# Input projection of a hybrid encoder layer: the last ten blocks as five pairs with seven products for eight, output gates stored to DRAM, second norms paced anew

## The chip, the cores and the metric

The kernel runs on one core of a Trainium2 chip. The metric is the time of one execution on the device in microseconds; the value compared is the median of the runs. The core's engines are TensorE (PE in the profile, its weight loads PEld), VectorE (DVE), ScalarE (ACT), GpSimd (POOL) and SyncE (SP), which issues nearly all DMAs.

## The reference

One layer of a chunk-causal encoder, on 1024 prompt tokens and 32 sample tokens (1056 columns, T) with 1024 features, in float32:

```python
h = rmsnorm(x, g_mix) * (1 + sc1) + sh1
u = h @ w_in
qa, ka, va, qm, km, vm, om, ip, fp, ga, gm = jnp.split(u, _split_points(), axis=-1)
ya = prompt_band_attention(qa, ka, va, rel_bias)       # 8 heads x 64
hm, (C1, n1, m1) = mlstm_chunkwise(q_m, k_m, v_m, log_i, log_f, C0, n0, m0, block)
ym = (head_rmsnorm(hm, mh_gain) * jax.nn.sigmoid(om)).astype(dt)   # 4 heads x 128
merged = (jax.nn.sigmoid(ga) * (ya @ w_br_att)
          + jax.nn.sigmoid(gm) * (ym @ w_br_mlstm))
x = x + gt1 * (merged @ w_out)
h2 = rmsnorm(x, g_ffn) * (1 + sc2) + sh2
g, up = jnp.split(h2 @ w_gate_up, 2, axis=-1)
x = x + gt2 * ((jax.nn.silu(g) * up) @ w_down)         # then a last rmsnorm
```

The change touches the columns `om` (512), `ga` and `gm` (1024 each) of `h @ w_in`, and the pace of `h2`'s norm.

## The kernel before, in words

Features lie on the partitions, tokens along the free axis, in three tiles of 352 (`TILES`). Every float32 operand is split into a high and a low part (`split_to`: ACT copies the high one, DVE or POOL subtracts for the low one), and a product is three passes (`PASSES`: high x high, low x high, high x low). `hs` holds the eight chunks of 128 features of `h`, split.

The input projection is cut into blocks of 128 output columns. A block calls `unit` once for each token tile: 8 chunks x 3 passes = 24 matmuls into one PSUM buffer from `mmt()` (three buffers, tag `mm`), and then ACT copies the buffer out: `om_block` into a slot (line 1324), `gate_block` into `raw` (line 747), which SP stores to `g_d` in DRAM. Other blocks serve attention, the convolution and the values of the mLSTM.

`segs` lists the blocks in seven segments. Beside the blocks of a segment runs a side job, a generator whose steps `Side.tick` calls in equal distances; `unit` ticks after every second chunk, that is every six matmuls. A side step issues its instructions at that place of the code: each engine but SP works in the order of the code. The last segment (index 6) has four `om_block`s and eight `gate_block`s; its job is the second half of the mLSTM, then `branch_operands`, with a delay of 13 ticks:

```python
ticks = sum(4 * run.w[2] for run in blocks)
delay = 13 if i >= 5 else 0
job = side.start(gen(), steps, ticks - delay - 4, delay)
```

The mLSTM goes over nine token blocks in steps: `first` (scores and transposes on PE, weights on DVE and ACT), `second` (four matmuls each with the state, the keys and the weights; ACT scales `num`, DVE adds and inverts, ACT squares) and, two iterations on, `third` (transposes into an `mm` buffer, copied out by ACT). The adaLN job (`ada_rest`, line 1298) runs beside all of it on DVE. `branch_operands` makes `ym` (sigmoid of `om` on ACT, line 1331; product with the mLSTM's output on DVE, line 1332; split) and `ya` (load of `ya_d`, line 1343; split). These go into the pool `slots`, 16 buffers of [128, 2, 1056]; `tmp` has four of [128, 1056].

`Weights` loads, splits and hands out the weights ahead of PE: `W.use` issues the splits of up to `W.ahead` blocks that fit in four split tiles (`wsp`), and loads three blocks ahead (`wraw`, three buffers).

After the projection the branches are merged with `sigmoid(ga)`, `sigmoid(gm)` from `g_d`. The output projection is partly in pairs of blocks with seven products for eight (`out_pair`, `half`, line 2011), whose results DVE adds to the residual (`take`, line 1946). `second_norm` makes `h2` beside it, for the first tile and then for the other two: `statistics` sums squares on PE (lines 1769, 1771), `spread` broadcasts the root, and then eight steps normalise one chunk each.

Of the kernel before, what the change touches and what calls it, by code (L numbers as in the profile page):

```python
# [17 lines left out]
P = 128  # L18
# [121 lines left out]
def hybrid_stream_step(  # L140
# [53 lines left out]
    def f(ap):  # L194
        return ap.bitcast(F32)
# [1114 lines left out]
    ADA_STEPS = 138  # L1310


    om = [None, None]
    ym, ya = [], []

    def om_block(b):
        w = w_cols(OM + b * P)

        def run():
            if b % 2 == 0:  # L1320
                om[b // 2] = slot([P, 2, T])
            for lo, hi in TILES:
                pt = unit(w, 0, hs, lo, hi)
                act.activation(om[b // 2][:, b % 2, lo:hi], pt, AF.Copy)
        run.w = w
        return run

    def branch_operands():
        for b in range(4):
            o = om[b // 2][:, b % 2]  # L1330
            act.activation(o, o, AF.Sigmoid)
            dve.tensor_tensor(o, o, hm_n[b // 2][:, b % 2], op=ALU.mult)
# [5 lines left out]
        if "ym" in dbg:  # L1338
            for h in range(MH):
                sp.dma_start(dbg["ym"][h], om[h // 2][:, h % 2])  # L1340
        for b in range(4):
            raw = tmpt()
            sp.dma_start(raw, ya_d[b])
            y = slot([P, 2, T], F32R)
            split_to(y, raw)
            ya.append(y)
            yield

    BR_STEPS = 12
# [22 lines left out]
    def open_mls():  # L1372
        att_cm.__exit__(None, None, None)
        mls_cm = tc.tile_pool(name="mls", bufs=2)
        mp_t.append(mls_cm.__enter__())
        mp_t.append(mls_cm)
        maskbig = mp_t[0].tile([P, P], F32, tag="maskbig", name="maskbig", bufs=1)
        pool.memset(maskbig, 0.0)
        pool.affine_select(out=maskbig, in_=maskbig, compare_op=ALU.is_ge, fill=BIG, base=0,
                           pattern=[[1, P]], channel_multiplier=-1)  # L1380
        masks.append(maskbig)

    def conv_rows():
        yield
        for out, j in ((new_conv_p, 0), (new_conv_s, 3)):
# [9 lines left out]
         lambda: attention(3), ATT_STEPS),  # L1395
        (open_mls, [vm_block(1), conv_block(2), conv_block(6), conv_block(3), conv_block(7)],
         lambda: mlstm(0), ML_STEPS),
        (nothing, [om_block(b) for b in range(4)] + b_gates(8, 16),
         lambda: chain(mlstm(1), conv_rows(), branch_operands()), ML_STEPS + BR_STEPS + 3),
    ]  # L1400

    for _, blocks, _, _ in segs:
        for run in blocks:
            W.add(run.w)


    class Seven:
# [610 lines left out]
    def out_pair(j, u):  # L2018
# [20 lines left out]
        if j == 1:  # L2039
# [592 lines left out]
```

## Time and profile before

| | |
|---|---|
| Median of 3 runs | 1580.81 us (1579.87 to 1581.0) |
| The profiled execution | 1580.16 us, of which the trace's span is 1578.4 us |
| Granted TensorE clock, mean | 0.999 |
| PE busy | 1558.0 us (99%), 10133 matmuls |
| DVE, ACT, POOL busy | 1133.5 (72%), 800.1 (51%), 422.7 (27%) us |
| First `om_block` | first evacuation at 545.9 us |
| Last `gate_block` | last evacuation at 701.8 us |
| HBM read, written | 149.06 MB, 34.17 MB |

Times in the profile are microseconds from the start of the span unless marked ns. A row names the line of the kernel, engine, operation, output <- input by the program's names, shape and count. In a list in order of time the first two columns are start and duration, and brackets give the time for which the engine was idle just before and what ended it. Matmuls are pipelined: the duration of one reaches into the next.

### The profile page before, as it was taken

Reading aid. Unit: us, or ns where it says so; the run is one execution under the profiler, and the core shown is the slowest. Engines: PE = TensorE matmul, PEld = TensorE weight load, DVE = VectorE, ACT = ScalarE, POOL = GpSimd, SP = SyncE. Lnnn points to the kernel's source line nnn. Section 1 sums busy time; section 2 is a strip of 40 time slices with the busy share of each in tenths; the row PEclk is TensorE's granted clock in tenths of the full one; section 3 lists DMA queues with packets and bytes.
Section 4 is the critical chain, followed back from the end, with each engine's and each line's share of the span. In section 5 each row is a group of like instructions: output and inputs, shape, how many; then the busy total and the mean of one; then the engine's idle time right before and its main releaser. Section 6 shows DMA issues by size and latency. Waiting matters only on the chain.

```text
span 1578.4 us, 27250 instructions
## 1 busy us (share of the span) xinstructions
PE 1558.0 (99%) x10133; PEld 1540.7 (98%) x10133; DVE 1133.5 (72%) x2346; ACT 800.1 (51%) x1756; POOL 422.7 (27%) x434
## 2 busy tenths in 40 slices
PE   8999999999999999999999999999999999999997
PEld 8999999999999999999999999999999999999997
DVE  3865565556766845546796799888888988799755
ACT  4765454544555545444454746544544445545443
POOL 0433343342223411000013100665665650000000
PEclk9999999999999999999999999999999999999999
DMA  9322233333132322573453312223222227427444
GB/s 375 128 78 83 89 97 103 97 131 108 42 91 74 85 81 86 126 233 131 128 163 123 108 55 68 82 69 103 72 82 95 68 78 256 143 81 244 139 135 159
DMA packets 173474, 184.99 MB, mean 117 GB/s; under 512 B 11830, under 2 KB 138458, under 8 KB 173214
## 3 DMA queue, kind: packets, MB, share of 16 engines
q1 hardware_dynamic: 171078, 182.13, 36.5%
q8 instruction: 80, 1.31, 0.3%
q10 hardware_dynamic: 2264, 1.13, 0.3%
q14 instruction: 52, 0.43, 0.1%
HBM read 149.06 MB, written 34.17 MB: 116 GB/s over the span
## 4 chain that ended last, share of the span: by engine, by line
PE 88%; DVE 5%; ACT 3%; DMA 2%; issue 1%; POOL 0%; DVEq 0%; SPq 0%; ACTq 0%; POOLq 0%
PE mm L418 37%; PE psb L2146 18%; PE mm L2146 11%; PE psb L2545 3%; PE mm L971 3%; PE mm L2545 2%; PE psV L876 2%; PE psb L2410 2%; PE mm L2011 2%; PE psS L817 1%; DMA s<-in_w_ada_dram 1%; PE psT L844 1%; PE mm L2410 1%; DMA s<-in_x_dram 1%; DVE st L831 1%
## 5 line engine op out<-in xcount | busy, mean ns | idle before, releaser
L418 PE MATMUL mm<-s,wsp 128*128 128x352 f32 x3720 | 625.2, 324 | 0.3 <-DVE s L688 0.3
L418 PEld LDWEIGHTS mm<-s,wsp 128*128 128x128 f32 x3720 | 595.5, 188 | 2.1 <-DVE s L688 0.5
L381 DVE TENSOR_TENSOR wsp<-wraw,wsp 128x512 fp32r<-128x512 f32 (+1 forms) x260 | 216.4, 849 | 94.5 <-ACT wsp L380 92.6
L2146 PE MATMUL psb<-s,wsp 128*128 128x352 f32 x1581 | 266.7, 322 | 0.0
L380 ACT ACTIVATE wsp<-wraw 128x512 fp32r<-128x512 f32 (+1 forms) x316 | 188.3, 617 | 136.2 <-PE psb L2146 42.0
L2146 PEld LDWEIGHTS psb<-s,wsp 128*128 128x128 f32 x1581 | 255.9, 188 | 0.0
L2146 PE MATMUL mm<-s,wsp 128*128 128x352 f32 x945 | 161.5, 322 | 0.7 <-DVE row L2184 0.7
L2146 PEld LDWEIGHTS mm<-s,wsp 128*128 128x128 f32 x945 | 153.2, 188 | 1.1 <-ACT wsp L380 1.0
L837 POOL TENSOR_SCALAR st<-st,mx 128x640 f32<-128x640 f32 (+5 forms) x72 | 53.2, 739 | 182.9 <-DVE mx L836 164.9
L1298 DVE CUSTOM_DVE_ANT_0 junk<-wa,t 128x512 bf16<-128x512 f32 x128 | 94.6, 739 | 2.5 <-DMA wa<-in_w_mod_dram 1.4
L381 POOL TENSOR_TENSOR wsp<-wraw,wsp 128x512 fp32r<-128x512 f32 x56 | 74.8, 1355 | 51.6 <-ACT wsp L380 49.3
L831 DVE CUSTOM_DVE_ANT_0 st<-psS,bias 128x640 f32<-128x640 f32 (+5 forms) x72 | 44.5, 618 | 57.9 <-PE psS L817 41.2
L832 ACT ACTIVATE st<-st,mx 128x640 f32<-128x640 f32 (+5 forms) x72 | 47.9, 666 | 63.7 <-DVE mx L831 63.5
L1961 POOL TENSOR_TENSOR t<-t,sl 128x352 f32<-128x352 f32 x19 | 22.7, 1198 | 207.2 <-ACT sl L1959 207.1
L851 ACT ACTIVATE pT<-psT 128x640 fp32r<-128x640 f32 (+3 forms) x80 | 38.6, 493 | 64.2 <-PE psT L844 49.8
L2518 POOL TENSOR_TENSOR fst<-fst,mhalf 128x6 f32<-128x6 f32 x1 | 2.2, 2247 | 235.2 <-DVE fst L2517 235.2
L856 DVE TENSOR_TENSOR pT<-psT,pT 128x640 fp32r<-128x640 f32 (+3 forms) x80 | 44.0, 558 | 21.5 <-ACT pT L851 21.5
L1511 POOL TENSOR_TENSOR wraw<-wraw,raw 128x512 f32<-128x512 f32 x33 | 55.8, 1702 | 0.9
L380 ACT ACTIVATE s<-x 128x352 fp32r<-128x352 f32 x84 | 37.5, 487 | 35.4 <-DVE x L1747 35.4
L971 PE MATMUL mm<-s,s 128*128 128x264 f32 (+3 forms) x432 | 54.5, 283 | 0.0
L2545 PE MATMUL psb<-s,wsp 128*128 128x352 f32 x330 | 54.1, 323 | 0.0
L2545 PEld LDWEIGHTS psb<-s,wsp 128*128 128x128 f32 x330 | 53.1, 188 | 0.1
(406 smaller groups left out, 2666.2 us busy)
## 6 DMA issues: line engine op xcount, KB each, us to landing
wraw<-in_w_in_dram SPq DMA_DIRECT2D x37, 512.0 KB, 3.7
wraw<-in_w_gate_up_dram SPq DMA_DIRECT2D x33, 512.0 KB, 4.1
wa<-in_w_mod_dram SPq DMA_DIRECT2D x64, 256.0 KB, 2.8
wraw<-in_w_down_dram SPq DMA_DIRECT2D x32, 512.0 KB, 4.1
a_d<-t SPq DMA_DIRECT2D x22, 528.0 KB, 2.7
g_d<-t SPq DMA_DIRECT2D x16, 528.0 KB, 3.4
t<-g_d SPq DMA_DIRECT2D x16, 528.0 KB, 4.6
s<-in_w_ada_dram SPq DMA_DIRECT2D x16, 512.0 KB, 7.9
```

The costliest lines, as they stand in the source:

```text
L380: act.activation(dst[:, 0], src, AF.Copy)
L381: eng.tensor_tensor(dst[:, 1], src, f(dst[:, 0]), op=ALU.subtract)
L418: pe.matmul(pt[:, :hi - lo], wt[(w0 + k) // 4][:, a, (w0 + k) % 4], xt[k][:, b, lo:hi], start=(k == 0 and q == 0), stop=(k == n - 1 and q ...
L831: dve.tensor_tensor_reduce(so, sv, bi, -1.0, 3.0e38, ALU.add, ALU.min, mx[:n, 1:2])
L832: act.activation(st[:n, :w], st[:n, :w], AF.Exp, bias=mx[:n, 1:2], scale=-1.0, accum_out=mx[:n, 2:3])
L837: pool.tensor_scalar(st[:n, :w], st[:n, :w], mx[:n, 3:4], 1.0, op0=ALU.mult, op1=ALU.mult)
L971: pe.matmul(pt[:n, :wd], hs[k][:, a, i * P:i * P + n], whl[b][:, k, :wd], start=(k == 0 and q == 0), stop=(k == KD - 1 and q == 2))
L1298: dve.tensor_tensor_reduce(junk, wa, crow[:, c], 1.0, 0.0, ALU.mult, ALU.add, at)
L1511: self.eng.tensor_tensor(a(dst), a(x), a(y), op=op)
L2146: pe.matmul(acc, wt[:, a, k], x[k][:, b], start=(start and not onto and k == 0 and q == 0), stop=(stop and k == 3 and q == 2), skip_group_ ...
L2410: pe.matmul(acc, wt[k // 4][:, u, k % 4], piece_of[k, i][:, v], start=(k == 0 and q == 0), stop=(k == KP - 1 and q == 2))
L2545: pe.matmul(acc, wt[(k - k0) // 4][:, u, (k - k0) % 4], piece_of[k, 2][:, v], start=(k == 0 and q == 0), stop=(k == NF - 1 and q == 2))
```

## The change

Om blocks 2 and 3, and for j = 4 to 7 the blocks j of `ga` and `gm`, become five pairs. In a pair, with its two weight blocks a and b, the feature chunks 0, 1, 4, 5 (`X`) on the token tiles 1 and 2 are a 2 x 2 by 2 x 2 product of blocks (each two chunks deep), done by seven products with sums of weights and of tokens instead of eight. Chunks 2, 3, 6, 7 (`R`), and tile 0, are multiplied as before. The token sums `T1` to `T4` are made once, beside om blocks 0 and 1 (`input_forms`: POOL joins high and low parts, DVE subtracts, ACT and DVE split), and live in a new pool `tf` of four buffers and in two slots. The weight sums are made by DVE for every pair.

A partial sum `u` stays in one PSUM buffer through the whole pair and is read after each of its products; `v` likewise for a shorter time. Om columns go to `om_d` in DRAM and are loaded again by `branch_operands`, one step ahead of their sigmoid. `W.ahead` is 4 from this segment on. The first `second_norm` waits one step less after its sums and makes 11 steps in 31 ticks with a delay of 1 (before: 12 in 28 with 2); the second starts one tick later.

```diff
     def om_block(b):
...
         def run():
-            if b % 2 == 0:
-                om[b // 2] = slot([P, 2, T])
+            raw = tmpt()
             for lo, hi in TILES:
                 pt = unit(w, 0, hs, lo, hi)
-                act.activation(om[b // 2][:, b % 2, lo:hi], pt, AF.Copy)
+                act.activation(raw[:, lo:hi], pt, AF.Copy)
+            sp.dma_start(om_d[b], raw)
...
     def branch_operands():
+        om = []
         for b in range(4):
-            o = om[b // 2][:, b % 2]
+            if b % 2 == 0:
+                om[:] = [slot([P, 2, T])]
+                sp.dma_start(om[0], om_d[b:b + 2].rearrange("n p t -> p n t"))
+                yield
+            o = om[0][:, b % 2]
             act.activation(o, o, AF.Sigmoid)
...
-    BR_STEPS = 12
+    def input_forms():
+        early, mid, late = [slice(lo, hi) for lo, hi in TILES]
+        places = [tf_pool[0].tile([P, 2, NT], F32R, tag="tf", name=nm("tf")) for _ in range(4)]
+        for n in (3, 1):
+            t = slot([P, 2, T], F32R)
+            places += [t[:, :, slice(lo, hi)] for lo, hi in TILES[:n]]
...
+        for p in range(2):
+            x = tmpt((P, 3, NT))
+            x0, x1, x2 = (x[:, i] for i in range(3))
+            whole(x0, p, mid)
+            whole(x2, p, late)
+            yield
+            whole(x1, p + 4, mid)
+            yield
+            minus(x2, x0, x2)
+            minus(x0, x1, x0)
+            yield
+            split("T1", p, x2)
+            minus(x1, x1, x2)
+            yield
+            split("T2", p, x1)
...
+    FORM_STEPS = 19
+    class InputSeven:
...
+            def sums():
+                x.append(tmpt((P, 4, 2, P)))
+                s1, s2, s3, s4 = (x[0][:, i] for i in range(4))
+                for o, u, v, op in ((s1, a(1, 0), a(1, 1), ALU.add), (s2, s1, a(0, 0), ALU.subtract),
+                                    (s3, a(0, 0), a(1, 0), ALU.subtract), (s4, a(0, 1), s2, ALU.subtract)):
+                    dve.tensor_tensor(o, u, v, op=op)
...
+    def input_pair(ca, cb, da, db):
...
+        def product(w, x, acc, i=0, start=True, stop=True, onto=False):
+            wt, = W.use(w)
+            n = len(x)
+            for k in range(n):
+                for q, (a, b) in enumerate(PASSES):
+                    pe.matmul(acc, wt[:, a, i + k], x[k][:, b], ...)
+                if k % 2 == 1:
+                    side.tick()
+            side.flush(1)
+            W.used(w)
+            return acc
...
+            u = product(aX, h((0, 1), t2), new())
+            copy(ra[:, t2], u)
+            c = product(aX, h(X, t0), new(), stop=False)
+            product(aR, h(R, t0), c, start=False)
+            copy(ra[:, t0], c)
+            c = product(aX, h((4, 5), t2), new(), 2, stop=False)
+            product(aR, h(R, t2), c, start=False)
+            add(ra[:, t2], c)
+            product(s12, F["T2"], u, 2, onto=True)
+            copy(ra[:, t1], u)
+            c = product(aR, h(R, t1), new())
+            add(ra[:, t1], c)
+            v = product(s12, F["T1"], new())
+            copy(rb[:, t1], v)
+            product(s34, F["T3"], u, onto=True)
+            add(rb[:, t1], u)
+            product(s34, h((4, 5), t1), v, 2, onto=True)
+            add(ra[:, t1], v)
+            sp.dma_start(da, ra)
+            c = product(bX, h(X, t0), new(), stop=False)
+            product(bR, h(R, t0), c, start=False)
+            copy(rb[:, t0], c)
+            product(bX, F["T4"], u, 2, stop=False, onto=True)
+            product(bR, h(R, t2), u, onto=True)
+            copy(rb[:, t2], u)
+            c = product(bR, h(R, t1), new())
+            add(rb[:, t1], c)
+            sp.dma_start(db, rb)
+        run.ticks = 23
...
+    BR_STEPS = 14
...
-        (nothing, [om_block(b) for b in range(4)] + b_gates(8, 16),
+        (nothing, [om_block(0), om_block(1), input_pair(OM + 2 * P, OM + 3 * P, om_d[2], om_d[3])]
+         + [input_pair(GA + j * P, GM + j * P, g_d[2 * j], g_d[2 * j + 1]) for j in range(4, 8)],
          lambda: chain(mlstm(1), conv_rows(), branch_operands()), ML_STEPS + BR_STEPS + 3),
...
+        if i == 6:
+            W.ahead = 4
+            side.start(input_forms(), FORM_STEPS, 21)
...
-            jobs.append(side.start(second_norm(parts[0], 2), 12, 28, 2))
+            jobs.append(side.start(second_norm(parts[0], 1), 11, 31, 1))
...
-                job = side.start(chain(second_norm(parts[1]), early_forms()), 9, 10)
+                job = side.start(chain(second_norm(parts[1]), early_forms()), 9, 10, 1)
```

More of the change, by code (lines that the diff above doesn't have):

```diff
@@ L1310, in hybrid_stream_step @@
     ADA_STEPS = 138
-    om = [None, None]
+    om_d = dr.tile([4, P, T], F32, name="om_d")
     ym, ya = [], []
@@ L1337, in branch_operands @@
             yield
-        if "ym" in dbg:
-            for h in range(MH):
-                sp.dma_start(dbg["ym"][h], om[h // 2][:, h % 2])
         for b in range(4):
@@ new lines, in hybrid_stream_step, with __init__, load, a @@
+    FORM_STEPS = 19
+    class InputSeven:
+        def __init__(self, ca, cb):
+            raw, x = [], []
+            def load(c):
+                raw.append(wraw.tile([P, KD, P], F32, tag="wraw", name=nm("wraw")))
+                sp.dma_start(raw[-1], in_block(c))
+            def a(i, h):
+                return raw[i][:, 4 * h:4 * h + 2]
+            def rows(i, g):
+                return raw[i].rearrange("p (h g k) c -> p h g k c", h=2, g=2)[:, :, g]
+            def sums():
[4 more added lines that the diff above has]
+                    dve.tensor_tensor(o, u, v, op=op)
+                return x[0][:, 0:2]
+            def block(src, uses, ld=lambda: None):
+                def split(_):
+                    t = wsplit_tile()
+                    v = src()
+                    hi, lo = (t[:, i].rearrange("p (h k) c -> p h k c", h=2) for i in range(2))
+                    act.activation(hi, v, AF.Copy)
+                    dve.tensor_tensor(lo, v, f(hi), op=ALU.subtract)
+                    return [t]
+                return [ld, split, uses, None, 1]
+            self.blocks = [
+                block(lambda: rows(0, 0), 3, lambda: load(ca)),
+                block(lambda: rows(0, 1), 3, lambda: load(cb)),
+                block(sums, 2),
+                block(lambda: x[0][:, 2:4], 2),
+                block(lambda: rows(1, 0), 2),
+                block(lambda: rows(1, 1), 3),
+            ]
@@ new lines, in input_pair, with h, new, run @@
+    def input_pair(ca, cb, da, db):
+        seven = InputSeven(ca, cb)
+        t0, t1, t2 = [slice(lo, hi) for lo, hi in TILES]
+        X, R = (0, 1, 4, 5), (2, 3, 6, 7)
+        def product(w, x, acc, i=0, start=True, stop=True, onto=False):
[3 more added lines that the diff above has]
+                for q, (a, b) in enumerate(PASSES):
+                    pe.matmul(acc, wt[:, a, i + k], x[k][:, b], start=(start and not onto and k == 0 and q == 0),
+                              stop=(stop and k == n - 1 and q == 2), skip_group_check=onto)
+                if k % 2 == 1:
[3 more added lines that the diff above has]
+            return acc
+        def h(ks, t):
+            return [hs[k][:, :, t] for k in ks]
+        def new():
+            return mmt()[:, :NT]
+        def run():
+            aX, aR, s12, s34, bX, bR = seven.blocks
+            F = forms_h
+            ra, rb = tmpt(), tmpt()
+            def add(o, y):
+                dve.tensor_tensor(o, o, y, op=ALU.add)
+            def copy(o, y):
+                act.activation(o, y, AF.Copy)
+            u = product(aX, h((0, 1), t2), new())
[26 more added lines that the diff above has]
+            sp.dma_start(db, rb)
+        run.blocks = seven.blocks
+        run.ticks = 23
+        return run
@@ L1376, in open_mls @@
         mp_t.append(mls_cm)
+        tf_cm = tc.tile_pool(name="tf", bufs=4)
+        tf_pool[:] = [tf_cm.__enter__(), tf_cm]
         maskbig = mp_t[0].tile([P, P], F32, tag="maskbig", name="maskbig", bufs=1)
@@ L1403, in hybrid_stream_step @@
         for run in blocks:
-            W.add(run.w)
+            for w in getattr(run, "blocks", None) or [run.w]:
+                W.add(w)
     class Seven:
@@ L1690, in hybrid_stream_step @@
         if gen is not None:
-            ticks = sum(4 * run.w[2] for run in blocks)
+            ticks = sum(getattr(run, "ticks", None) or 4 * run.w[2] for run in blocks)
             delay = 13 if i >= 5 else 0
@@ L1699, in hybrid_stream_step @@
     side.flush()
+    tf_pool[1].__exit__(None, None, None)
     mp_t[1].__exit__(None, None, None)
```

27 lines of the change are left out of this document (added).

## The prediction

> **What bounds the kernel now.** I read the busy shares first, then the stretches of time, then the waits of TensorE (PE) in the one stage that the change rewrites, then the engines in order of time around one step there.
>
> ```profile
> PE 1558.0 (99%) x10133; PEld 1540.7 (98%) x10133; DVE 1133.5 (72%) x2346; ACT 800.1 (51%) x1756; POOL 422.7 (27%) x434
> ...
> L418 PE MATMUL mm<-s,wsp 128*128 128x352 f32 x3720 | 625.2, 324 | 0.3 <-DVE s L688 0.3
> ```
>
> ```profile
> 541.90:701.60 159.70, 159.70 (x1046) 158.23 (x1046) 83.71 (x212) 73.51 (x177) 16.27 (x25) 1.00 0.45 127
> ```
>
> ```profile
> 800.00:900.00 100.00, 98.64 (x625) 97.67 (x624) 76.75 (x153) 57.49 (x110) 25.86 (x22) 1.00 0.48 150
> ```
>
> ```profile
> 1000.00:1100.00 100.00, 100.00 (x624) 100.00 (x624) 88.99 (x126) 48.55 (x93) 62.11 (x40) 1.00 0.29 91
> ```
>
> The page first: PE is busy 99% of the span. The three rows after it give busy time by stretch (the engines in the order PE, weight load, DVE, ACT, POOL, with the count of instructions). 541.9 to 701.6 us is the last segment of the input projection, where all edits but the norm ones lie: PE is busy in 159.70 of 159.70 us, ACT in 73.51, DVE in 83.71. So a matmul less there is time less, as long as nothing new makes PE wait.
>
> The 324 ns in the L418 row is not what a matmul costs: matmuls overlap. 1000 to 1100 holds 624 of the 128x352 form in 100.00 us of busy PE, 0.160 us each. That is the price used.
>
> **What is taken away.** A plain block costs 8 chunks x 3 passes x 3 tiles = 72 matmuls, a pair of blocks 144. The new pair's products, in units of six matmuls: one for `u`, then 2+2+1+2+1+2+1+1+1 up to `s34`'s second use, then 2+2+1+2+2: 23 units, 138 matmuls. Five pairs save 30 matmuls: 30 x 0.160 = 4.8 us. The work that the blocks bring to ACT and DVE (six half-size splits and six evacuations instead of eight and six; five additions of 352 and four sums per pair) fits their free time above; only its place in their queues matters.
>
> **Where PE will wait.** Each engine keeps the order of the code. One tick of the side jobs comes after every six matmuls (0.96 us). The mLSTM job now makes 43 steps in 139-13-4 = 122 ticks, from tick 13: step n falls on the first tick at or past 13 + 2.84n. Om blocks 0 and 1 take ticks 1 to 24, pair p starts after tick 24 + 23p. The old numbers, 41 in 127, put the first `second()` (step 6) on tick 32.
>
> In a pair the tight spot is `v`: `s12`x`T1` goes to `v` (tick 12 of the pair), ACT copies `v` to `rb`, and `s34`xchunks 4, 5 is added onto `v`. Between them PE has only `s34`x`T3`, six matmuls, 0.96 us. A hand-over and return cost, from the output projection, where DVE evacuates between products:
>
> ```profile
> 827.93 0.58 DVE L1946 SCALAR_TENSOR_TENSOR x<-mm,amod,x 128x352 f32<-128x352 f32 x1
> ...
> 828.73 4.03 PE L2011 MATMUL mm<-s,wsp 128*128 128x352 f32 x24
> ```
>
> ```profile
> 844.13 2.08 PE L2011 MATMUL mm<-s,wsp 128*128 128x352 f32 x12
> ...
> 844.33 0.58 DVE L1946 SCALAR_TENSOR_TENSOR x<-psT,amod,x 128x352 f32<-128x352 f32 x1 [0.76 <-PE psT L2011]
> ```
>
> PE's next product starts at 844.13, the evacuation of the last at 844.33: 0.20 us. DVE ends at 828.51, PE goes on at 828.73: 0.22. With a copy of 0.44 that makes 0.86 us, just inside 0.96, if ACT is free. It isn't where a side step has queued work ahead of the copy. The product's tick runs before the copy is issued, and by the formula step 8 falls on tick 36 (pair 0, tick 12) and step 16 on tick 59 (pair 1, tick 12). Both are `second()`, seen here once in the kernel before (in order of time, all engines):
>
> ```profile
> 600.04 3.15 PE L418 MATMUL mm<-s,wsp 128*128 128x352 f32 x18
> ...
> 600.32 0.63 ACT L1211 ACTIVATE num<-psT,wc 128x129 f32<-128x129 f32 x2 [1.92 <-PE psT L1207]
> ...
> 601.83 0.17 DVE L1225 RECIPROCAL dn<-dn 128x2 f32<-128x2 f32 x1
> 601.91 0.67 DVE L1298 CUSTOM_DVE_ANT_0 junk<-wa,t 128x512 bf16<-128x512 f32 x1
> 602.11 0.40 ACT L1228 ACTIVATE sq<-num,dn 128x128 f32<-128x128 f32 x1 [1.16 <-DVE dn L1225]
> ...
> 603.04 0.44 ACT L747 ACTIVATE t<-mm 128x352 f32<-128x352 f32 x1
> ```
>
> PE has done with the step at 600.04, where the unit goes on. ACT scales `num`, waits for DVE's sum and reciprocal (601.83), squares twice, and only at 603.04 comes to the evacuation queued behind, which ends at 603.48: 3.44 us. Nobody minded, for the next unit had another PSUM buffer. In the pair, PE goes on 3.44 + 0.22 = 3.66 us after the step, has 0.96 us of its own, and waits 2.7. Twice: **+5.4 us**. Bounds: from ACT's first start to the copy's end (600.32 to 603.48, 3.16 us, no hand-over) 2.4 each; with one DVE addition (0.5 us) queued ahead 3.2: 4.8 to 6.4.
>
> **PSUM.** There are three `mm` buffers; `u` holds one for the whole pair, `v` another for part. `third()` needs one too. In pair 1, tick 3, it and the running `c` fill the rest, and the next product waits until ACT has been through `first()` and `third()`'s copies; in pair 2, tick 14, `u`, `v` and `third()` leave none until DVE has added `v`. By hand-over plus one operation, 0.2 + 0.5 + 0.2 less the little PE has of its own, about 0.7 us each: **+1.4** (0, if a buffer is free earlier, to 2).
>
> **Output gates by way of DRAM.** Four stores of 528 KB leave nothing waiting: `raw` has four buffers. Two loads of 1056 KB come back, with ACT's sigmoid one step, 2.8 ticks, behind each. The nearest row is the load of the attention output, behind which ACT's split stands directly:
>
> ```profile
> t<-ya_d SPq DMA_DIRECT2D x4, 528.0 KB, 5.3
> ```
>
> ```profile
> 682.50 0.46 ACT L747 ACTIVATE t<-mm 128x352 f32<-128x352 f32 x1 [1.36 <-PE mm L418]
> 688.58 1.09 ACT L380 ACTIVATE s<-t 128x1056 fp32r<-128x1056 f32 x1 [5.62 <-DMA t<-ya_d]
> ```
>
> ```profile
> 658.34 1.08 ACT L1331 ACTIVATE s<-s 128x1056 f32<-128x1056 f32 x1
> ...
> 659.46 1.26 DVE L1332 TENSOR_TENSOR s<-s,s 128x1056 f32<-128x1056 f32 x1 [1.01 <-ACT s L1331]
> ```
>
> (KB and median us from issue to landing; ACT alone; the old kernel's sigmoid and product.) ACT stood 5.62 us for the load and PE lost nothing: a unit is 24 matmuls, 3.85 us, and three buffers turned. Now the copies behind such a wait free the one or two buffers that `u` and `v` leave. Load 0-1 is issued at the end of pair 2, its sigmoid is queued after 18 matmuls of pair 3 (2.9 us), and PE needs the first buffer back after 54 (8.6 us), the second after 66 (10.6). With 5.3 us to landing (for twice the bytes I allow 8, an estimate), sigmoid 1.08, DVE's product 1.26, split 1.09, second sigmoid and product, `c'` is added at 10.6 to 14.6 us. **+1.5** (0 to 4); the load of 2-3 has more room.
>
> **Slots.** The sums' forms hold two of 16 slots to the end of the segment. hs 8, forms 2, ym 4, ya 2: the third `ya` finds none until `s34`x`T3` of the last pair has been read. Its ACT split (step 40, tick 127 = pair 4, tick 11) stands ahead of that pair's copy of `v`: 0.25 + 1.09 + 0.44 + 0.22 after that product: **+2.0** (1 to 3.5, if its data is late too). The `ya` splits before it wait for their loads as in the old kernel.
>
> **First 21 ticks.** 19 steps of forms: POOL 8 sums of 352, DVE 18 operations, ACT 8. DVE was full there already:
>
> ```profile
> 541.90:557.30 15.40, 15.40 (x98) 15.40 (x97) 14.11 (x26) 7.28 (x12) 7.62 (x6) 1.00 0.44 130
> 557.30:580.00 22.70, 22.70 (x152) 22.70 (x152) 6.44 (x20) 9.05 (x23) 1.22 (x4) 1.00 0.24 73
> ```
>
> ```profile
> 708.19 0.52 DVE L381 TENSOR_TENSOR s<-t,s 128x352 fp32r<-128x352 f32 x1 [0.56 <-ACT s L380]
> ```
>
> DVE is busy 14.11 us in 15.40, then 6.44 in 22.70. One subtraction of 352 columns takes 0.52 us: 18 x 0.52 = 9.4 us of DVE work fit in there only by running late into pair 0, whose `s12` split must be done 42 matmuls, 6.7 us, after its start: **+1.0** (0 to 4).
>
> **Norms.** PE's waits in the stretch 800 to 900, all in PE's order of time:
>
> ```profile
> 869.03 2.17 PE L2011 MATMUL psS<-s,wsp 128*128 128x352 f32 x12 [0.31 <-DVE x L1946]
> 871.75 2.18 PE L2011 MATMUL mm<-s,wsp 128*128 128x352 f32 x12 [0.55 <-DVE x L1946]
> ...
> 883.12 0.38 PE L1771 MATMUL psV<-ones,sl 128*128 128x1 f32 x2 [0.40 <-ACT sl L1959]
> ```
>
> 0.31 + 0.55 + 0.40 = 1.26 us, nearly all of the 1.36 that this stretch lacks. The first norm now steps 11 in 31 ticks instead of 12 in 28, thinner on DVE, whose `take` PE waited for; the second starts a tick (0.96 us) later, which covers the 0.40. **-0.7**; -1.3 if all go, +1.0 if the shifted steps meet other takes.
>
> **Sum.** -4.8 + 5.4 + 1.4 + 1.5 + 2.0 + 1.0 - 0.7 = +5.8 us on the profiled execution's 1580.16 us (its span is 1578.4). That execution is 0.65 below the median of 1580.81, so 1586.6 for the median. All low ends: -0.3, 1580.5; all high ends: +16.1, 1596.9.
>
> **Rivals.** *Even.* Only the two chains bite, the rest is hidden: -4.8 - 0.7 + 5.4 = -0.1, about 1580.7. For it: PE waits nowhere in the 159.7 us now, so the schedule has slack I may undercount. *Faster.* The copy of `v` is free in time, because the step's chain on ACT is done before PE has left the two small products: 1575.3 with nothing else, 1576 with a little. It decides at 0.96 us: chain, copy and return together must stay below it; the row above says 3.66. That the change does not save its matmuls is excluded by the count. *Worse.* POOL's sums hold DVE up for their whole length:
>
> ```profile
> 545.39 1.66 DVE L1298 CUSTOM_DVE_ANT_0 junk<-wa,t 128x512 bf16<-128x512 f32 x1
> ```
>
> ```profile
> 543.21 3.29 POOL L381 TENSOR_TENSOR wsp<-wraw,wsp 128x512 fp32r<-128x512 f32 x2 [7.61 <-ACT wsp L380]
> ```
>
> ```profile
> L1961 POOL TENSOR_TENSOR t<-t,sl 128x352 f32<-128x352 f32 x19 | 22.7, 1198 | 207.2 <-ACT sl L1959 207.1
> ```
>
> The operation that took 0.67 us above takes 1.66 at 545.39, while POOL's L381 runs. Eight sums, 1.2 us each by the mean of the last row, would put 9.6 us more on DVE; pair 0 would start some 10 us behind, and PE lose about 5 us more than forecast: 1592. The Trainium skill has such a rule (SBUF — State Buffer, "Who interferes with whom"): two of those ports are shared by DVE and POOL under an exclusive lock, and the loser waits for the whole instruction. By that rule the worse case would be the forecast; the one row agrees with it, and no row here shows a DVE operation held by a sum of this size.
>
> **Chances.** Forecast 0.50 (its own range 1582.5 to 1594: the sum with single terms at their ends), even 0.27, faster 0.13, worse 0.10. 0.2% is 3.2 us, about what a measurement here tells from no change. Slower by more than that (over 1584): the worse case, most of the forecast's, 0.58. Faster (under 1577.6): 0.14. Same: 0.28. Range: 1577 to 1594 leaves out most of "faster" below and, above, the ends of the forecast and of the worse case.
>
> **What would show it.** 30 fewer 128x352 matmuls on PE. In pairs 0 and 1, PE idle about 2.7 us before the products onto `v`, released by ACT's copy; in pair 4 about 2 us at the same place; less than 1 us at the head of pair 0 and in pair 3. The waits of 869 to 883 gone or moved. Wrong, if PE's first wait on `v` is under 1 us, or if PE stands idle in the two om blocks.

## The result, and the profile after

The changed kernel takes 1596.13 us (median, 1594.89 to 1596.27) against 1580.42 for the kernel before in the same comparison: ratio 1.0099, 95% interval 1.0087 to 1.011. It is 15.7 us slower; the forecast was 5.8, and the time lies 2 us above the range.

The page after: busy time, and the group of the pairs' matmuls (busy us, mean ns of one, idle time just before them and what ended most of it).

```profile
PE 1559.7 (98%) x10103; PEld 1538.7 (97%) x10103; DVE 1173.1 (74%) x2419; ACT 808.6 (51%) x1774; POOL 425.6 (27%) x440
...
L1465 PE MATMUL mm<-s,wsp 128*128 128x352 f32 x630 | 112.9, 331 | 13.5 <-ACT t L1488 6.8
```

The 30 matmuls are gone (10133 to 10103), and PE is busy longer all the same. The last segment of the projection, and the stretch of it that holds pair 3:

```profile
541.90:716.84 174.94, 160.83 (x1015) 156.13 (x1014) 117.92 (x284) 83.37 (x196) 21.25 (x31) 0.98 0.49 137
```

```profile
661.00:702.00 41.00, 41.00 (x257) 41.00 (x257) 30.37 (x58) 22.18 (x32) 0.00 (x0) 1.00 0.63 205
```

Before, the segment took 159.70 us with PE busy throughout; now 174.94, of which PE is busy 160.83. That is 15.2 of the 15.6 us by which the span grew. From 661 to 702, where om comes back from DRAM, PE doesn't stand at all. Its waits in the segment, from PE's order of time:

```profile
569.49 4.71 PE L1465 MATMUL mm<-s,wsp 128*128 128x352 f32 x18 [2.48 <-ACT t L1323]
574.36 0.46 PE L1172 MATMUL psS<-s 128*128 128x128 f32 x2 [0.16 <-DVE W L1190]
...
589.52 3.37 PE L1465 MATMUL mm<-s,wsp 128*128 128x352 f32 x12 [2.26 <-ACT t L1488]
...
604.72 1.23 PE L1465 MATMUL mm<-s,wsp 128*128 128x352 f32 x6 [0.61 <-DVE t L1485]
...
612.82 1.23 PE L1465 MATMUL mm<-s,wsp 128*128 128x352 f32 x6 [0.81 <-ACT s L1244]
...
620.59 2.19 PE L1465 MATMUL mm<-s,wsp 128*128 128x352 f32 x12 [1.42 <-DVE t L1485]
...
628.61 2.22 PE L1465 MATMUL mm<-s,wsp 128*128 128x352 f32 x12 [2.49 <-ACT t L1488]
...
654.89 2.19 PE L1465 MATMUL mm<-s,wsp 128*128 128x352 f32 x12 [0.71 <-ACT s L1244]
...
660.76 4.11 PE L1465 MATMUL mm<-s,wsp 128*128 128x352 f32 x24 [0.56 <-ACT s L1244]
...
702.88 0.75 PE L1465 MATMUL mm<-tf,wsp 128*128 128x352 f32 x3 [0.44 <-DVE t L1485]
...
707.11 5.07 PE L1465 MATMUL mm<-s,wsp 128*128 128x352 f32 x30 [2.04 <-ACT t L1488]
```

In brackets stands what the prediction priced: the head of pair 0 (2.48 and 0.16), the copy of `v` in pairs 0 and 1 (2.26, 2.49), the short waits round `third()` in pairs 1 and 2 (0.61, 0.81, 1.42, 0.71, 0.56), the slot in pair 4 (2.04); 0.44 behind DVE's addition is new (the addition stood behind DVE's split of a `ya`, 701.14 to 702.31). Together 14.0 us.

Two things are in no bracket. First, the same number of matmuls takes unequal time: 12 take 3.37 us at 589.52 and 2.22 at 628.61. The granted clock (third number from the right) tells why:

```profile
569.70:573.12 3.42, 3.42 (x13) 3.42 (x13) 3.04 (x9) 3.41 (x8) 0.00 (x0) 0.50 0.37 84
573.12:576.53 3.41, 3.25 (x22) 2.99 (x21) 2.83 (x9) 1.46 (x5) 0.00 (x0) 1.00 0.91 200
590.18:593.60 3.42, 3.42 (x15) 3.42 (x14) 3.42 (x9) 0.88 (x2) 0.00 (x1) 0.50 0.33 106
624.31:627.73 3.42, 1.81 (x14) 1.52 (x12) 2.66 (x11) 1.14 (x5) 0.00 (x0) 1.00 0.70 223
```

Twice the clock falls to half for 3.41 us, which costs about 1.7 us each (half of 3.41, an estimate). Second, a stopped PE must be filled again: six matmuls start at 565.78, at 0.160 the next were due at 566.74, and it starts at 569.49: 2.75 us lost where the bracket says 2.48, 0.27 more. For the 11 waits listed that is 3.0 us, an estimate from this one.

The account: -4.8 (matmuls) + 14.0 + 3.4 (half clock) + 3.0 (refill) - 0.5 (norms) = 15.1; the span grew by 15.6. Busy PE checks the two estimates: 160.83 against 159.70 - 4.8 is 5.9 us more, where they say 6.4. The norms' term is PE's idle time there: 0.31 + 0.55 + 0.40 = 1.26 before, now 0.19 (884.17), 0.26 (898.32) and a new 0.31 behind DVE's split L381 (986.78), together 0.76.

The step behind one of these waits, all engines in order of time:

```profile
585.69 0.61 PE L1207 MATMUL psT<-s,W 128*128 128x129 f32 x4
...
586.05 0.73 PE L1465 MATMUL mm<-tf,wsp 128*128 128x352 f32 x3
...
586.34 0.63 ACT L1211 ACTIVATE num<-psT,wc 128x129 f32<-128x129 f32 x2 [1.67 <-PE psT L1207]
...
587.84 0.17 DVE L1225 RECIPROCAL dn<-dn 128x2 f32<-128x2 f32 x1
588.10 0.40 ACT L1228 ACTIVATE sq<-num,dn 128x128 f32<-128x128 f32 x1 [1.14 <-DVE dn L1225]
...
589.03 0.44 ACT L1488 ACTIVATE t<-mm 128x352 f32<-128x352 f32 x1
```

This is the predicted chain, operation by operation: `v` is complete on PE at about 585 (its last three matmuls run from 584.32 to 584.96), and its copy stands behind `num`, DVE's reciprocal and two squares until 589.03.

At the head of pair 0 it is another chain, here on ACT alone:

```profile
568.59 0.50 ACT L1367 ACTIVATE s<-t 128x352 fp32r<-128x352 f32 x1 [2.48 <-DVE t L1379]
568.99 0.45 ACT L1323 ACTIVATE t<-mm 128x352 f32<-128x352 f32 x1
```

The copy of om block 1 (L1323) that PE waits for at 569.49 stands behind a split of the token sums (L1367), and that one behind DVE.

### The profile page after: what moved, and what is told of

Same layout as the page of the kernel before. It is cut to its first block, busy times and chain, and to the rows that moved or that the text cites. A ratio compares the mean times of both kernels' runs of the same rounds, so it can differ in the third digit from the quotient of the medians.

```text
span 1594.0 us, 27324 instructions
## 1 busy us (share of the span) xinstructions
PE 1559.7 (98%) x10103; PEld 1538.7 (97%) x10103; DVE 1173.1 (74%) x2419; ACT 808.6 (51%) x1774; POOL 425.6 (27%) x440
## 4 chain that ended last, share of the span: by engine, by line
PE 78%; DVE 10%; ACT 6%; issue 2%; DMA 2%; POOL 1%; SPq 0%; DVEq 0%; ACTq 0%; POOLq 0%
PE mm L418 23%; PE psb L2327 18%; PE mm L2327 11%; PE mm L1465 4%; PE psb L2726 3%; PE mm L971 3%; PE mm L2726 2%; PE psV L876 2%; PE psb L2591 2%; PE mm L2192 2%; PE psS L817 1%; PE psT L844 1%; DMA s<-in_w_ada_dram 1%; PE mm L2591 1%; DVE s L2036 1%
## 5 line engine op out<-in xcount | busy, mean ns | idle before, releaser
L418 PEld LDWEIGHTS mm<-s,wsp 128*128 128x128 f32 x3000 | 480.4, 188 | 1.8 <-DVE s L688 0.5
L2327 PE MATMUL psb<-s,wsp 128*128 128x352 f32 x1581 | 266.7, 322 | 0.0
L2327 PEld LDWEIGHTS psb<-s,wsp 128*128 128x128 f32 x1581 | 255.9, 188 | 0.0
L381 DVE TENSOR_TENSOR wsp<-wraw,wsp 128x512 fp32r<-128x512 f32 x242 | 206.6, 868 | 50.6 <-ACT wsp L380 48.9
L380 ACT ACTIVATE wsp<-wraw 128x512 fp32r<-128x512 f32 (+1 forms) x296 | 176.8, 616 | 132.1 <-PE psb L2327 37.5
L2327 PEld LDWEIGHTS mm<-s,wsp 128*128 128x128 f32 x945 | 153.1, 188 | 1.9 <-ACT wsp L380 1.0
L1465 PEld LDWEIGHTS mm<-s,wsp 128*128 128x128 f32 x630 | 103.7, 193 | 16.3 <-ACT t L1488 7.7
L381 POOL TENSOR_TENSOR wsp<-wraw,wsp 128x512 fp32r<-128x512 f32 x54 | 71.7, 1347 | 45.2 <-ACT wsp L380 42.9
```

Of the source, the lines that this page charges most:

```text
L380: act.activation(dst[:, 0], src, AF.Copy)
L381: eng.tensor_tensor(dst[:, 1], src, f(dst[:, 0]), op=ALU.subtract)
L418: pe.matmul(pt[:, :hi - lo], wt[(w0 + k) // 4][:, a, (w0 + k) % 4], xt[k][:, b, lo:hi], start=(k == 0 and q == 0), stop=(k == n - 1 and q ...
L1465: pe.matmul(acc, wt[:, a, i + k], x[k][:, b], start=(start and not onto and k == 0 and q == 0), stop=(stop and k == n - 1 and q == 2), ski ...
L2327: pe.matmul(acc, wt[:, a, k], x[k][:, b], start=(start and not onto and k == 0 and q == 0), stop=(stop and k == 3 and q == 2), skip_group_ ...
```

## The experiments

All are the changed kernel with the edit shown, unless another base is named; times stand against about 1580.1 us for the kernel before. A profile is of one execution, and the executions of one kernel spread, from 1594.89 to 1596.27 for the change and from 1592.99 to 1596.43 for the first edit below; so a median 1 or 2 us below the change's shows little by itself, and the single edits are judged by the waits in their traces.

**The copy of v first.** `product` gets a hook that runs ahead of the tick:

```diff
-            v = product(s12, F["T1"], new())
-            copy(rb[:, t1], v)
+            v = new()
+            product(s12, F["T1"], v, then=lambda: copy(rb[:, t1], v))
```

> The copy of v is issued ahead of the tick that follows s12 x T1, nothing else moves. Theory (ACT's queue: the step of the side job, queued ahead of the copy, is what PE waits for): the three waits on the copy, 2.26 + 2.49 + 2.04 = 6.8 us, go; with them 0.27 us each for refilling PE (565.78 + 6 x 0.160 = 566.74, next start 569.49: 2.75 lost, 2.48 idle), and the half clock after the one at 589.5 (1.6 us): 6.8 + 0.8 + 1.6 = 9.2, time about 1587. Rival (PE's own 0.96 us is too short for any hand-over and return there): 0.5 to 1 us is left at each of the five v, time 1589 to 1591. Rival (ACT is late as a whole in pairs 0 and 1): the wait moves to the next product that needs ACT, time 1593 to 1596.

Measured 1594.62 (1592.99 to 1596.43). PE's waits in pairs 0, 1 and 4:

```profile
592.50 0.44 PE L1242 MATMUL mm<-ident,num 128*128 128x128 f32 x2 [2.04 <-DVE t L1487]
...
630.68 0.44 PE L1242 MATMUL mm<-ident,num 128*128 128x128 f32 x2 [1.62 <-DVE t L1487]
...
706.51 6.60 PE L1465 MATMUL mm<-s,wsp 128*128 128x352 f32 x30 [2.04 <-ACT t L1490]
```

The wait at the product onto `v` is gone, and 2.04 and 1.62 us have come back a few matmuls later: `third()` wants an `mm` buffer, and the buffer of `v` is only free when DVE has added it, behind the same step's work. The last-named rival was right. In pair 4 the split that waits for the slot is issued a tick earlier than this edit reaches; here it also met the half clock (30 matmuls in 6.60 us, 5.07 before).

**The token sums in 30 ticks instead of 21.**

> The 19 steps of the token sums are spread over 30 ticks instead of 21. Theory (the evacuation of om block 1 stands on ACT behind splits that wait for DVE and POOL): the wait of 2.48 us at the head of pair 0 goes, with 0.27 us of refill and the 1.7 us of half clock behind it: 4.5 us less, time about 1591.6. Rival (DVE has too much work altogether in these 45 us, and only the place is paid): PE stands for 2 us or more in pair 0 ahead of s12 x T2, T1 or s34 x T3, time 1594 to 1598.

Measured 1595.07 (1593.17 to 1596.98). The wait of 2.48 at 569.49 is gone, and one of 2.58 stands a product later, behind DVE's weighting of the scores (L1190). So DVE is late at either pace of the sums. Why it is late this run doesn't show; the median is 1.1 us below the change's, within the spread.

**third() in psV.** `pt = ps_v() if pr else mmt()` in `third()`.

> third() of the second mLSTM half transposes into the psV buffer instead of an mm buffer. Theory (PSUM: u, v and third() leave none of three mm buffers): the five short waits of pairs 1 and 2, 0.61 + 0.81 + 1.42 + 0.71 + 0.56 = 4.1 us, go, with 5 x 0.27 us of refill: 5.5 less, time about 1590.6. Rival (the two that DVE's addition ends are DVE's lateness, not a want of buffers): only 0.81 + 0.71 + 0.56 + 3 x 0.27 = 2.9 go, time 1593.2. Rival (psV is no freer): new waits of second() on ACT's copies, time 1596 or more.

Measured 1594.79 (1594.2 to 1595.68). All five short waits are gone, so they were a want of `mm` buffers, those that DVE's addition ended too. But PE reaches the copy of `v` in pair 1 that much earlier, and waits there 3.86 us instead of 2.49. At the head of pair 0 this execution had no half clock; PE waits 2.49 us and then, for DVE, once more:

```profile
574.31 0.46 PE L1172 MATMUL psS<-s 128*128 128x128 f32 x2 [1.73 <-DVE W L1190]
```

In the change the same group starts at 574.36, after 2.48 us, half clock and 0.16 us. So DVE sets the time there, and the half clock of the change only fills a wait of 1.6 us.

**Token sums on DVE instead of POOL.** `whole` with `dve.tensor_tensor`.

> The eight sums of high and low token parts run on DVE instead of POOL. Theory of the one engine's load: DVE gets 8 x 0.52 = 4.2 us more in the first 21 ticks, is later still, and the wait at the head of pair 0 grows from 2.5 to 4 to 6.5 us: time 1598 to 1600. Rival (the worse case of the prediction: a sum on POOL holds DVE up for its whole length): DVE's operations there take their usual time again, the wait at the head shrinks below 1.5 us, time 1594 or less.

Measured 1593.28 (1590.34 to 1594.42): 2.9 us below the change's median with more work on the fuller engine, and each of its executions is faster than each of the change's. First the kernel after, then this one, DVE and POOL alone:

```profile
558.85 3.82 POOL L1376 TENSOR_TENSOR t<-s 128x352 f32<-128x352 f32 x3 [4.73 <-DVE s L1127]
...
560.43 2.79 DVE L1440 TENSOR_TENSOR wsp<-wraw,wsp 128x512 fp32r<-128x512 f32 x2
```

```profile
558.99 1.28 DVE L1440 TENSOR_TENSOR wsp<-wraw,wsp 128x512 fp32r<-128x512 f32 x2
```

Beside POOL's sums the same two subtractions took 2.79 us, without them 1.28: 1.5 us more of DVE's time (2.2 with the split before them, 1.26 against 0.52). This is the mechanism of the prediction's rival *worse*, though not its size: it had 1.2 us of DVE for each of the eight sums, and three ran here. The Trainium skill (SBUF — State Buffer, "Who interferes with whom") says that a DVE instruction with two inputs in SBUF contends with a GpSimd instruction that reads SBUF. These rows agree. Beside that, DVE had stood 2.98 and 0.99 us for POOL's results in the change; how the gain divides between the two the run doesn't show. What is left at the head is 1.73 us.

**Both locks on the ring at once**, the copy of `v` first and `third()` in psV:

> Both at once: the copy of v ahead of the tick, and third() in psV. In each run alone the wait came back at the other's place (2.04 and 1.62 us ahead of third()'s transposes in the one, 3.86 instead of 2.49 us ahead of the product onto v in the other). Theory (two locks on the same ring of three mm buffers, each of which suffices to hold PE until the step's chain has gone through ACT and DVE): together the seven waits of pairs 0 to 2, 0.61 + 0.81 + 1.42 + 0.71 + 0.56 + 2.26 + 2.49 = 8.9 us, go, with 7 x 0.27 of refill and on average one half clock of 1.6: 12.4 less, time about 1584. Rival (DVE and ACT are too full in these pairs, and the ring only shows it): at least 3 us come back ahead of a c or u product, time 1588 or more.

Measured 1589.73 (1588.52 to 1591.19): 6.4 less than the change, where the two alone gave 1.5 and 1.3. What returned:

```profile
594.80 0.71 PE L1205 MATMUL psV<-s,kw 128*128 128x129 f32 x4 [1.09 <-ACT s L1244]
...
629.12 0.71 PE L1205 MATMUL psV<-s,kw 128*128 128x129 f32 x4 [2.09 <-ACT s L1244]
```

`second()` now stands for psV until ACT has copied `third()` out.

**adaLN resting in the om blocks** (`ada[1] = 0.0`, then `rate * 139 / 115`).

> The adaLN job rests during om blocks 0 and 1 and runs 139/115 as fast in the pairs. It takes 10 x 0.76 us of DVE there. Theory (DVE's backlog at the head of pair 0 is all of its work: taps, sums, splits, adaLN): the wait of 2.48 and the 0.16 behind it fall below 0.5 us, with refill and half clock 4.0 less, time about 1592, and the later pairs show no new wait. Rival (the eight sums on POOL, for which DVE stands 2.98 + 0.99 us and which slow its operations, set the end by themselves): 1.5 us or more of wait is left at the head, time 1594 to 1595.

Measured 1602.39 (1599.63 to 1602.76), 6 us worse than the change. The wait at the head moved to 572.40 (2.34 us), and the hurried job ran into its own loads: PE stood 4.84 us in pair 2 for `num`, which DVE could not scale while it waited 5.35 us for `wa`.

**Five edits together**: the four above that had helped or might (copy first, psV, sums on DVE, adaLN at rest), and the splits of the third and fourth `ya` one step behind their loads.

> Five edits: copy of v ahead of the tick, third() in psV, token sums on DVE, adaLN resting in the om blocks, and the third and fourth ya loaded a step before their split, so that their slots are asked for after s34 x T3. Theory (all of PE's waits in the segment come from these four places): PE waits less than 1 us in all of the segment, nothing is left of the half clocks, and the 30 matmuls and the norms remain: 1580.1 - 4.8 - 0.7 = 1574.6, 1574 to 1577. Rival (the full DVE): with 4.2 us of sums more and adaLN squeezed into the pairs, PE waits 3 us or more, 1578 to 1584.

Measured 1589.68 (1589.32 to 1590.48). DVE and SP in order of time:

```profile
639.96 0.34 SPq L1160 DMA_DIRECT2D out_dram<-C  x1
...
645.20 0.34 SPq L1281 DMA_DIRECT2D wa<-in_w_mod_dram  x1
```

```profile
651.50 0.69 DVE L1298 CUSTOM_DVE_ANT_0 junk<-wa,t 128x512 bf16<-128x512 f32 x1 [4.77 <-DMA wa<-in_w_mod_dram]
```

The load of `wa` follows the stores of the mLSTM's state, which take 11.9 us to land, and itself takes 6.3 (2.8 in the median of such loads in the changed kernel). That the stores are what delays it is inferred from this order. PE's wait of 4.28 us there brought half clock from 650.3 to 657.1. `second()` stands for psV here too, 1.09, 2.07 and 0.45 us, so the theory had overlooked a place. In pair 4 the wait for the slot is gone; 1.80 us behind DVE's addition stand in its place, which the hurried adaLN probably delays.

**The clock.** In the kernel before, PE transposes a tile that POOL has copied one to four times, twelve times in the segment:

```diff
+        pz = mmt()
+        for _ in range((1, 2, 3, 2, 4, 1, 3, 2, 3, 4, 2, 3)[i // 2 % 12]):
+            z = mp_t[0].tile([P, 352], F32, tag="stall", ...)
+            pool.tensor_scalar(z, src, 1.0, 1.0, ...)
+        pe.transpose(pz[:, :P], z[:, :P], ident)
```

> The kernel before with waits put in on purpose: after every second token tile of the om blocks and the gate blocks 8 to 15, PE transposes a tile that POOL has copied one to four times over, some twelve waits of 1 to 6 us. Theory (the clock looks at a fixed grid of windows of 3.41 us, and halves itself for the next window when PE stood for about two thirds of one): each drop to half lasts 3.4 us and starts on one grid, whatever the length of the wait; waits over 5.5 us always give one, waits under 2.2 us never, and between them it depends on where the wait lies in the grid. Rival (length alone: a drop right behind every wait over about 2.3 us, the two waits of 2.49 and 2.04 us without one being chance): every wait over 2.5 us is followed by half clock from its first matmul on.

One execution, 1630.25 us. The drops start at 577.88, 594.95, 612.01, 639.32, 656.39 and 714.4, all multiples of 3.413 us apart, as are the two of the changed kernel (590.18 - 569.70 = 6 x 3.413). Stretches that are windows of this grid, with PE's busy time and then the clock; after the first four rows two of ahead_four (below) and two of ada_pause, on the grids of their own drops:

```profile
652.97:656.39 3.42, 1.52 (x12) 0.87 (x10) 0.34 (x3) 2.72 (x10) 1.43 (x4) 1.00 0.00 0
656.39:659.80 3.41, 1.20 (x5) 1.20 (x6) 3.34 (x7) 0.41 (x1) 2.15 (x3) 0.50 0.63 204
724.65:728.06 3.41, 1.54 (x10) 1.54 (x11) 2.62 (x3) 2.24 (x4) 1.43 (x2) 1.00 0.43 165
728.06:731.47 3.41, 3.41 (x23) 3.41 (x22) 0.12 (x1) 0.47 (x1) 0.00 (x0) 1.00 0.99 297
```

```profile
613.85:617.26 3.41, 1.57 (x11) 1.32 (x10) 1.97 (x5) 2.37 (x7) 0.89 (x2) 1.00 0.03 2
617.26:620.68 3.42, 3.42 (x16) 3.42 (x15) 2.04 (x6) 2.19 (x6) 0.00 (x0) 0.50 0.86 293
```

```profile
623.59:627.00 3.41, 1.50 (x11) 1.21 (x10) 1.82 (x8) 1.63 (x7) 0.00 (x0) 1.00 0.53 156
627.00:630.42 3.42, 3.04 (x21) 2.96 (x22) 2.54 (x6) 1.49 (x3) 0.89 (x2) 1.00 0.00 0
```

In this run a window with PE idle for 1.90 us (3.42 - 1.52) was followed by half clock, one with 1.87 was not. That is no sharp bound: 1.84 us (3.41 - 1.57) was followed by half clock in ahead_four, 1.91 was not in ada_pause. Over the segment's windows in the thirteen runs that had a drop, 1.99 us or more at full clock was always followed by half clock, 1.74 or less never, and between them either came; the ends of matmuls are modelled in the profile, so hundredths mean little. The rival falls: a wait of 2.52 us, split by the grid into 1.63 and 0.89, had no drop behind it, nor had the 2.49 of the changed kernel (1.61 in the window 624.31 to 627.73). The theory's bounds for the waits fall too, since the 1.84 of ahead_four is below its 2.2. So a wait of 2.5 us costs 2.5 or 4.2, by where it happens to lie, and the refill beside it. The Trainium skill (TensorE: Matmul & The Clock Gate, Part 1) states a free-running window of 3413 ns and a fall of the clock after at least one idle window. The grid here agrees with the window; for the fall 1.84 us of one, 54%, was enough.

**third() in psS.** The copy first, sums on DVE, the late `ya`, and `pt = (a[i][0] if i < NB else ps_s())[:, 2 * P:]`; and the same with om blocks 2 and 3 plain and the sums started later (`FORM_STEPS, 34, 8`).

> Copy of v ahead of the tick, token sums on DVE, third and fourth ya split later, and third() in free columns of psS (256 to 511 of the buffer that first() has just written) instead of psV, where second() stood behind its copies for 1.09 and 2.09 us. adaLN as it was. Theory (the waits come from the ring of mm buffers, the slot, and DVE's backlog at the head): of 14 us of waits the one at the head is left with 1.7 us, some 0.4 behind DVE's additions in the last pair, refill of 0.5 and at most half a drop of the clock: 1580.1 - 4.8 - 0.7 + 1.7 + 0.4 + 0.5 + 0.5 = 1577.7, 1576.5 to 1579.5. Rival (ACT and DVE are too slow for pairs 0 to 2 by themselves, whatever buffer third() has): 3 us or more of new waits in pairs 0 to 2, 1581 or more.

> As four_edits, and om blocks 2 and 3 stay plain (six matmuls more): the token sums get 34 ticks from the eighth on, behind DVE's work on the convolution, and are first needed at tick 57. Theory (the wait at the head is DVE's backlog of these 30 us alone): it goes, and the time is 1580.1 - 24 x 0.160 - 0.7 + 0.6 = 1576.2, 1575 to 1577.5. Rival (the sums only push the backlog into the next blocks): 1.5 us or more of wait before the first pair's products, 1578 or more.

Measured 1604.69 (1603.89 to 1607.03) and 1604.59 (1604.22 to 1605.33). A row of the first:

```profile
592.07 0.69 PE L1242 MATMUL psS<-ident,num 128*128 128x128 f32 x2 [4.13 <-ACT kw L1184]
```

Six such waits, 1.49 to 4.13 us: the transposes now wait until ACT has read the rest of the buffer (`kw`), behind the exponential that waits for DVE. The edit made its own wait, so neither theory is tested, but for one thing: with the sums started later no wait was left at the head.

**Two parts of the change alone, in the kernel before**: om by way of DRAM, all blocks plain, and the norms' pace.

> The kernel before with two parts of the change alone: om through DRAM (all om blocks plain) and the norms' new pace. Theory (the trace after shows no wait at the loads of om, and the waits of 869 to 883 shrunk): -0.7, 1579.4. Rival (the prediction's terms: +1.5 for the loads of om, -0.7): 1580.9.

Measured 1580.27 (1579.76 to 1580.62), ratio 1.0001 (0.9992 to 1.0009). PE doesn't wait in the segment. In the stretch 800 to 900 PE is busy 99.43 us instead of 98.64:

```profile
800.00:900.00 100.00, 99.43 (x631) 98.73 (x631) 77.25 (x152) 57.54 (x111) 25.60 (x22) 1.00 0.48 149
```

The two waits for `take` and the one for `sl` shrink from 1.26 to 0.43 us, but a new one of 0.33 stands behind them, at 971.19 for DVE's split (L381). The 0.5 us that are left are too small for the times. The loads of om cost nothing here; but with all blocks plain the three buffers turn as before, so it is the changed kernel's stretch 661 to 702 that answers the prediction's term.

**The order on ACT.** In the second half of the mLSTM, `third()` is issued ahead of `first()`:

> The changed kernel, but in the second mLSTM half third() is issued ahead of first() in its step, so that its copies stand ahead of first()'s exponential and scaling on ACT; it stays in an mm buffer. Theory (third()'s buffer is held because its copies queue behind first(), whose exponential waits for DVE: 1.90 us at 603.99, 2.33 at 621.09): the waits released by L1244 and the two by L1485 in pair 1, 0.61 + 0.81 + 1.42 + 0.71 + 0.56 = 4.1 us, go with 1.35 of refill: 5.5 less, 1590.6. Rival (three mm buffers are too few with u and v in two, whatever the order): the waits stay within 1 us in sum, 1595 to 1597; or the time comes back at the copies of v, as in third_pv (1594.8).

Measured 1595.82 (1594.52 to 1596.3). The waits in pair 1 shrink to 0.35 and 0.16, and the one for the copy of `v` grows to 3.26, as in psV; those of pair 2 (0.72, 0.56) stay. Alone it is worth nothing.

**All places at once**: copy first, `third()` ahead and in psV, sums on DVE, late `ya`; and the same with om blocks 2 and 3 plain and the sums later.

> All five pairs with copy of v ahead of the tick, third() ahead of first() and in psV, token sums on DVE, third and fourth ya split later; adaLN as it was. Theory (each wait of the segment has its own place in a queue or ring): psV's waits of 1.09 and 2.09 us go, left are 1.7 at the head, 0.4 in the last pair, 0.5 of refill and half a drop of the clock (0.8): 1580.1 - 4.8 - 0.7 + 1.7 + 0.4 + 0.5 + 0.8 = 1578. Rival (pairs tie PE to the chain through ACT and DVE as such): 3 us or more of waits in pairs 0 to 2, 1581 or more.

> As ahead_five, with om blocks 2 and 3 plain and the token sums in 34 ticks from the eighth on. Theory: the head's wait goes as it did in four_pairs, no drop of the clock is left: 1580.1 - 24 x 0.160 - 0.4 + 0.6 = 1576.5, 1575 to 1578. Rival as for ahead_five: 1580 or more.

Measured 1579.43 (1578.08 to 1580.25), ratio 0.9996 (0.9987 to 1.0005), and 1581.18 (1580.27 to 1582.37). The first takes 16.7 us off the change. Its waits are 1.40 (head), 0.20 and 0.48, and its profile has no drop of the clock; the segment ends 1.9 us earlier than before: 4.8 - 2.08 - 3 x 0.27. One more wait, 0.39 behind DVE, stands just after the segment (706.06). The second lost the wait at the head. But its first pair starts a tick later against the mLSTM, `second()` comes ahead of `s12` x `T1` instead of behind it, and the copy of `v` stands behind the chain once more: 1.84 us at 615.93, with half clock after it.

**adaLN's share at the head.** On top of the five edits, adaLN rests in om block 1 and makes up in pairs 3 and 4; or it runs 495/470 as fast from its start and rests in om blocks 0 and 1:

```diff
-            ada = side.start(ada_rest(), ADA_STEPS, 495)
+            ada = side.start(ada_rest(), ADA_STEPS, 470)
...
+            rate, ada[1] = ada[1], 0.0
...
+            if i == 6 and n == 2:
+                ada[1] = rate
```

> ahead_five, and the adaLN job rests during om block 1 (3.3 steps, 2.5 us of DVE) and makes them up in pairs 3 and 4, behind the stores of the mLSTM's state that held its loads up in ada_pause. Theory (the last wait at the head, 1.40 us for W behind DVE's backlog, is a matter of these microseconds): it goes with its 0.27 of refill, 1579.4 - 1.7 = 1577.8, 0.15% below the kernel before. Rival (adaLN made up in pairs 3 and 4 costs as much there, at DVE's additions): 1579.4.

> ahead_five, and adaLN runs 495/470 as fast from its start and rests in om blocks 0 and 1 (6.7 steps, 5.1 us). Theory: the wait of 1.40 goes as in ahead_rest1, and nothing is to be made up in the pairs: 1577.5. Rival (its loads meet the stores of the state at another phase, or attention feels DVE): a wait of 3 us or more in pair 2 or in the attention segments, 1580 or more.

Measured 1584.51 (1578.79 to 1586.31) and **1577.68** (1577.17 to 1578.12; ratio 0.9984, 0.9976 to 0.9993). The first shifts the loads of `wa` behind the state's stores (DVE waits 3.19 us for one), and what is made up probably delays the last pair (1.34 us behind DVE's addition there, 2.03 just after the segment). The second has one wait left in the segment:

```profile
600.04 0.44 PE L1242 MATMUL psV<-ident,num 128*128 128x128 f32 x2 [0.20 <-DVE C L1216]
```

It beats both kernels: 2.4 us faster than the kernel before. The new pace of adaLN was not run in the kernel before; but there PE waits for nothing between 420 and 868 us, so that the pace alone has nothing to gain in this stretch.

## Why the prediction was right and wrong

The direction and the mechanism were right: PE, which never waited in this segment, now waits for ACT and DVE through `u`, `v` and `third()`, and that outweighs 30 matmuls. By its steps:

- *Matmuls*, -4.8: right. The end of the segment in ahead_five comes out with them to the tenth.
- *The copy of v*, +5.4: 2.26 + 2.49 + 2 x 0.27 = 5.3, at the two places named. But the step is not removed by moving the copy; `v` is held by DVE's addition too.
- *Slots*, +2.0: 2.04 at the place named, gone when the splits come later.
- *PSUM*, +1.4: failed. There were five waits, 4.1 us, not two. The estimate took one operation and a hand-over; in the trace `third()`'s copies stand behind `first()`, whose exponential waits for DVE (1.90 us at 603.99). third_ahead shows this for the three of pair 1, which shrink from 2.84 to 0.51 us, not for the two of pair 2; third_pv shows the want of buffers for all five.
- *First 21 ticks*, +1.0, at most 4: failed in place and size. The prediction had PE wait for the split of `s12`. PE waits for an `mm` buffer of om block 1, whose copy stands on ACT behind a split of the token sums that waits for DVE (568.59 above). 2.48 + 0.16, refill and half clock make 4.6. That exceeds the bound. POOL's sums slowed DVE, which the prediction had as a rival at 0.10; sums_dve gained 2.9 us, the slowing and DVE's waits for POOL's results together. That this rival's 1592 lay nearer to the result than the forecast is luck: it had DVE lose 9.6 us to eight sums, where beside three of them DVE lost 2.2.
- *om by DRAM*, +1.5: failed. In 661 to 702 PE is busy throughout. The loads took longer than estimated (9.8 us median to landing, estimate 8), but none of the four sigmoids (672.46, 676.39, 683.76, 690.32) shows a wait for one; the copies that the bound had queued behind the load never did. (The prediction's times of 10.6 to 14.6 us there come to 11.1 to 13.8 by its own figures up to the second product, or 0.5 more with the addition; nothing hangs on it.)
- *Norms*, -0.7: right in direction, 0.5 by idle time. The three waits shrank from 1.26 to 0.45 us, and a new one of 0.31 behind DVE's split took part of it back, which the prediction had not; the times can't tell.
- *Not in the sum at all*: refill, 3.0 us, and half clock, 3.4, by the estimates; 5.9 together by busy PE. Both come with waits, and the sum priced waits by their idle time only. Of the half clock 1.6 us at the head fill a wait that DVE sets anyhow (third_pv). The 4.3 to 4.8 us that are left are the largest part of the miss of 9.5; behind them come the head (4.2 us of waits at full clock in third_pv, against 1.0) and PSUM (4.1 against 1.4).

The rival *even* rested on the slack of the kernel before. That slack was three buffers turning; `u` and `v` take it away. The terms also don't add up one by one: single cures gave 1.5, 1.1, 1.3, 2.9 and 0.3 us (all but the 2.9 within the spread of the executions), two of them together 6.4, and the set 16.7, since PE that arrives earlier at the next lock waits there. What stays open is how much of the 2.4 us of the last kernel would outlast another phase of the side jobs: ahead_four shows that one tick brings a wait back.

## What to carry to other kernels

Price a wait of TensorE at its idle time plus the refill (0.27 us here), and, where some 1.8 us of idle time can fall into one window of 3.4 us, at the chance of half clock in the next. When a product chain is held in PSUM across other work, list every engine operation that must read the buffer, and what stands ahead of each in its queue; curing one lock shows the next, so cure them together before judging the idea. A side job that is paused or hurried changes which transfers its loads meet.

## What the runs showed of the hardware beyond that

- The granted clock is decided per window of a fixed 3.413 us grid: at full clock 1.99 us or more of idle PE in a window halved it for the next, 1.74 or less did not, and from 1.84 to 1.91 both came. In a window at half clock less is enough to keep it there: 1.44 us idle (639.32 to 642.73 in the run with inserted waits) and 0.88 us (635.44 to 638.85 in four_pairs) were followed by another at half, 0.69 (594.95 to 598.36, inserted waits) was not. So the way up asks for more.
- A POOL sum of 352 columns took 1.1 us in the mean of the eight, on DVE 0.5; beside it two DVE subtractions went from 1.28 to 2.79 us.
- Stores of the mLSTM's state, two of 64 KB and two of 0.5 KB, took 11.9 us to land, and a 256 KB load issued behind them 6.3 us (all5).
